# The inverse chains spaced evenly over the heads with the gate's blocks moved between them; the last two attention heads with more columns and their work shared out

## The chip, the cores and the metric

The kernel runs on one core of one Trainium2 chip. The metric is the device time of one execution in microseconds (us). The engines are TensorE (PE, with its weight loads PEld), VectorE (DVE), ScalarE (ACT), GpSimd (POOL) and SyncE (SP), which issues most DMAs. Each engine works through its own instructions in order.

## The reference

A two-layer encoder trunk over 1280 tokens of width 1024: 1024 prompt tokens and 256 sample tokens. Layer 0 is a neighbourhood attention of 16 heads of 64, its output gated by silu; layer 1 is a bidirectional gated DeltaNet of 8 heads in chunks. Cut to what matters:

```python
# layer 0, per head: window of keys, bias, softmax, weighted values; then the gate and the output projection
p = softmax(where(mask, q @ k.T + bias, NEG_INF)); o = p @ v
x = x + (o * silu(g)) @ w_out
# layer 1: projections, centred depthwise conv of 5 taps and silu on q, k, v (32 blocks of 128 channels)
proj = h @ w_in
qkv = silu(conv5(proj[..., :4096])); z = proj[..., 4096:6144]; beta, decay = ...
# per head and chunk of 64 tokens, in both directions
a_kk = tril_strict((k*beta) @ k.T * decay)
w, u = solve(I + a_kk, k*beta*exp(g)), solve(I + a_kk, v*beta)
# scan over the chunks: v_new = u - w @ S; o = q @ S + a_qk @ v_new; S = S*exp(g_last) + k.T @ v_new
y = x + (rmsnorm(o) * silu(z)) @ w_out     # then a last RMSNorm
```

## The kernel before, in words

Channels lie on partitions, tokens along the free dimension, in three token blocks of 512, 512 and 256 columns (b = 0, 1, 2). Each projection is done with weights and inputs split in a high and a low part: `proj_steps` issues for each of 8 slices of the width three matmuls (high by high, high by low, low by high, line L1176), so a block of 128 channels is 72 matmuls of 30,720 columns. `T` is 1280, `NP` 1024, `KD` 8.

The stages, by the profiled execution: attention and its output projection to about 770 us; `gdn_proj` from 770 to 1600; a transition to 1640, in which the scan's first operands are loaded (`kT`, `qT`, `vT`, L813 and on) and the last gate half runs; the scan to about 2030; the last projection and norm.

What runs beside what is set by `Side`: a generator of a piece of work is added with a delay and a pace, both counted in columns of the projection matmuls that go on meanwhile. At each projection matmul `tick(n)` adds its columns; a generator whose due time has come is advanced by one step, and its next due time is what it yields times its pace. The program so written is then laid out in a fixed order per engine, which a scheduler may still change locally, except where `keep_in_program_order` holds an instruction in its place.

**Attention.** Head h's `attention` generator (scores, softmax, transposes, product with V, gate) runs beside the projections for head h+1 (`qk_head`), the values (`v_quad`) and the gate (`g_pair`). In head 15 the projection beside it is the output projection w_o, on the part of its input that is there: `o_part(b, k)` loads what two earlier heads left in DRAM, copies it to a high part `OH` and subtracts this to get the low part `OL` (lines L337 and L340). `softmax` is a sum with a minimum on DVE (L216), an exponential on ACT (L217), a reciprocal (L218) and a scale by it (L219) on DVE. L236 transposes, L240 and L241 split the result, L256 multiplies by V, L262 to L264 apply the gate.

**gdn_proj.** 32 blocks of q, k and v channels run one after the other, f = 4h + ch: ch 0 is q, 1 is k, 2 and 3 are the halves of v. They come in the order k of head 0, then q, v, v of head h and k of head h+1. After each, ACT copies PSUM to `raw` (L487) and scales the middle tap (L490), DVE does four multiply-adds (L492), ACT a tanh (L495), DVE a product (L496), and SP stores the result (`qkv_spill`). In what follows f(h,ch) is such a block.

When a k block is there, the head's **inverse chain** `invert` is added (chain h). Its steps, in order:

- three rounds of: decay matmuls (L557), their masks on DVE (L560), exponential on ACT (L563), a store (`e_spill`), k by k matmuls on `th` (L581), DVE's products (L587, L589);
- D on ACT and DVE (L595, L596), its transpose (L605) and a mask (L606) on DVE;
- a substitution of 30 steps, each a product (L611) and a sum (L613) on DVE;
- two transposes on DVE (L617, L618), then copies into M on ACT (L626, L627) and into W and WT on POOL (L632 to L634);
- after a yield of 34000 columns the matmuls L639 of the inverse with M, ACT's copies (L642), the matmuls L646, copies on DVE (L648 to L652), matmuls L659 and L667, a copy on DVE (L669) and the store of W (`w_spill`, L670).

A chain yields 146,000 columns in all, 114,000 of them ahead of L639. The gate z of the scan's output is 16 half blocks of 128 channels, `gate_z`: projection, tanh (L519), product on DVE (L522), store (`z_spill`). In the kernel before, a chain starts 26000 columns after it is added, at pace 1 (0.92 for head 7), and after it the two z halves of head h-1 follow; z(7,0) is the last block of `gdn_proj`, and z(7,1) runs in the transition.

Of the kernel before, what the change touches and what calls it, by code (L numbers as in the profile page):

```python
# [11 lines left out]
AF = mybir.ActivationFunctionType  # L12
OP = mybir.AluOpType
# [22 lines left out]
def layer0(ctx, tc, a, h1_out):  # L36
    nc = tc.nc
# [5 lines left out]
    XH, XL = parts(xp)  # L43
# [6 lines left out]
    pp, pv = (x0.enter_context(banks(tc, n, b, "right")) for n, b in (("rms0_ps", 2), ("v0", 6)))  # L50
# [80 lines left out]
    P, V = {}, {}  # L131
# [41 lines left out]
    with st:  # L173
# [36 lines left out]
                nc.scalar.activation(G[b], t, AF.Tanh, scale=0.5)  # L210
                nc.vector.scalar_tensor_tensor(G[b], G[b], 1.0, t, op0=OP.add, op1=OP.mult)

        def softmax(S, bias, Pv):

            mx = ap.tile([128, 4], F32, name="mx", bufs=4)
            nc.vector.tensor_tensor_reduce(Pv, S, bias, -1.0, 3e38, OP.add, OP.min, mx[:, 0:1])  # L216
            nc.scalar.activation(Pv, Pv, AF.Exp, scale=-1.0, bias=mx[:, 0:1], accum_out=mx[:, 1:2])  # L217
            nc.vector.reciprocal(mx[:, 2:3], mx[:, 1:2])  # L218
            nc.vector.tensor_scalar(Pv, Pv, mx[:, 2:3], None, op0=OP.mult)  # L219

        def turned(units):

# [43 lines left out]
        def attention(h, qkk, V, G, O):  # L266

            Q, KH, KL = qkk
            bt = ap.tile([128, 896], F32, name="bias", bufs=2)
            nc.sync.dma_start(bt, a["bias_p"][h])  # L270

            def scores(p):
                own = {}
                for m in (2 * p, 2 * p + 1):
                    k0, k1 = max(m - 1, 0), min(m + 2, 8)
                    n = 128 * (k1 - k0)
                    S = ps_s.tile([128, 512], F32, name="S")[:, :n]
                    q = Q[:, 128 * m:128 * m + 128]
                    nc.tensor.matmul(S, q, KH[:, 128 * k0:128 * k1], start=True, stop=False)
                    nc.tensor.matmul(S, q, KL[:, 128 * k0:128 * k1], start=False, stop=True)  # L280
                    P = ap.tile([128, 384], F32, name="P", bufs=3)
                    b0, _ = BIAS[0 if m == 0 else 2 if m == 7 else 1]
                    softmax(S, bt[:, b0:b0 + n], P[:, :n])
                    for s in range(k0, k1):
                        own[s, m] = P[:, 128 * (s - k0):128 * (s - k0) + 128]
                    yield 800
                m = 2 * p
                edge = [(s, 128 * i, [own[s, m + i]]) for s, i in ((m - 1, 0), (m + 2, 1)) if (s, m + i) in own]
                return [[(s, 0, [own[s, m], own[s, m + 1]])] for s in (m, m + 1)] + [edge]

            def scores_s():
                bs = ap.tile([128, 2, 256], F32, name="bias_s", bufs=1)
                nc.sync.dma_start(bs, a["bias_s"][h])
                Ps = ap.tile([128, 2, 256], F32, name="Ps", bufs=1)
                S = ps_s.tile([128, 512], F32, name="S").rearrange("p (g n) -> p g n", g=2)
                for g in range(2):
                    q = Q[:, NP + 128 * g:NP + 128 * g + 128]
                    nc.tensor.matmul(S[:, g], q, KH[:, NP:], start=True, stop=False)
                    nc.tensor.matmul(S[:, g], q, KL[:, NP:], start=False, stop=True)
                    softmax(S[:, g], bs[:, g], Ps[:, g])  # L300
                yield 1600
                return [[(8 + s, 0, [Ps[:, g, 128 * s:128 * s + 128] for g in range(2)])] for s in range(2)]

            def products(j, units, ts):
                while not (j // 2 in G and all(s in V for us in units for s, _, _ in us)):
                    yield 400
                g = G[j // 2][:, 256 * (j % 2):256 * (j % 2) + 256]
                if j < 4:
                    rows = lambda t: t.rearrange("p (c r) -> p c r", r=16)
                    o = O[:, :NP].rearrange("p (r c) -> p c r", c=64)[:, 16 * j:16 * j + 16]  # L310
                    yield from pv(units, ts, V, h % 4, o, rows(g), rows)
                else:
                    yield from pv(units, ts, V, h % 4, O[:, NP:], g, lambda t: t)
                done[h] += 1

            last = None
            for j in range(5):
                units = yield from (scores(j) if j < 4 else scores_s())
                if last:
                    yield from products(*last)  # L320
                else:
                    yield 3200
                ts = yield from turned(units)
                last = j, units, ts
            yield 1600
            yield from products(*last)
            if h % 2 and h < 15:
                nc.sync.dma_start(a["o_dram"][h // 2], O)

        def o_part(b, k, late=False):  # L330

            t0, n = BLK[b]
            t = O[:, t0:t0 + n]
            if k < KD - 1:
                t = OL[k][b].bitcast(F32)
                nc.sync.dma_start(t, a["o_dram"][k, :, t0:t0 + n])
            high = nc.scalar.activation(OH[k][b], t, AF.Copy)  # L337
            if late:
                tc.keep_in_program_order(high)
            (nc.vector if k % 2 else nc.gpsimd).tensor_sub(OL[k][b], t, OH[k][b])  # L340

        done = {}
        side = Side()
        a["hi"] = True
        qkk = qk_head(0)
# [4 lines left out]
        for h in range(16):  # L350
            done[h] = 0
            G = GS[h // 2]
            V = nV if h % 4 == 0 else V
            side.add(attention(h, qkk, V, G, O), 2000, 0.75 if h in (0, 14, 15) else (1.6, 1.5, 1.5, 1.35)[h % 4])
            side.tick(0)
            q = (h + 1) // 4
            if h % 4 == 0:
                v_quad(q, V, [s for s in (4, 5) if s not in V], side)
            if h < 15:
                qkk = qk_head(h + 1, side)  # L360
            else:
                wo = [load_w(tc, a, a["w_o"][i]) for i in range(2)]
                OH, OL = parts(xp)
                begun = {(i, b): pmm.tile([128, 512], F32, name="mm")[:, :BLK[b][1]]
                         for i, b in ((0, 0), (1, 0), (0, 2))}
                for k in range(KD + 1):
                    if k < KD - 1:
                        o_part(0, k, True)
                        o_part(2, k, True)
                    if k > 1:  # L370
                        for i, b in begun:
                            for n in proj_steps(nc, begun[i, b], *wo[i], OH, OL, b, [k - 2]):
                                side.tick(n)
            if h % 4 == 0:
                v_quad(q, V, [s for s in range(10) if s not in V], side)
            if h % 4 in (1, 2) and h < 14:
                p = h // 2 + 1
                g_pair(p, GS[p], range(3), side)
            elif h % 4 == 3 and h < 15:
                nV = {}  # L380
                v_quad(q, nV, range(4), side)
            side.drain()
            if h % 2 and h < 15:
                O = ap.tile([128, T], F32, name="O", bufs=1)
# [55 lines left out]
def gdn_proj(tc, a, pmm, XH, XL):  # L440

    nc = tc.nc
    with ExitStack() as st:
# [27 lines left out]
        Z = ap.tile([128, NB, 128], F32, name="Z", bufs=1)  # L471
        for t in (D, W, WT):
            nc.gpsimd.memset(t, 0.0)
        for h, ch in [(0, 1)] + [(h + (ch == 1), ch) for h in range(8) for ch in (0, 2, 3, 1)][:-1]:
            f = 4 * h + ch
            wh, wl = a["first"].pop(0) if a["first"] else load_w(tc, a, a["w_qkv"][f])
# [20 lines left out]
            nc.sync.dma_start(a["qkv_dram"][f, :, :NP], th[:, :NP])  # L497
            nc.sync.dma_start(a["qkv_dram"][f, :, NP:], th[:, NP + 2:])
            if ch == 1:
                side.add(invert(tc, a, ap, pp, h, th, D, W, WT, Z), DELAY, 0.92 if h == 7 else 1)  # L500
            if ch == 1 and h:
                gate_z(tc, a, pmm, XH, XL, h - 1, side)
        gate_z(tc, a, pmm, XH, XL, 7, side, (0,))
        side.drain()


DELAY = 26000


def gate_z(tc, a, pmm, XH, XL, h, side, halves=(0, 1)):  # L510

    nc = tc.nc
    ws = [load_w(tc, a, a["w_z"][2 * h + i]) for i in halves]
    for i, (wh, wl) in zip(halves, ws):
        for b, (t0, n) in enumerate(BLK):
            ps = pmm.tile([128, 512], F32, name="mm")[:, :n]
            proj(nc, ps, wh, wl, XH, XL, b, side)
            z = a["zp"].tile([128, 512], F32, name="z")[:, :n]
            tanh = nc.scalar.activation(z, ps, AF.Tanh, scale=0.5)  # L519
            if h == 7:  # L520
                tc.keep_in_program_order(tanh)
            nc.vector.scalar_tensor_tensor(z, z, 1.0, ps, op0=OP.add, op1=OP.mult)  # L522
            nc.sync.dma_start(a["z_dram"][2 * h + i, :, t0:t0 + n], z)
# [907 lines left out]
```

## Time and profile before

| what | us |
|---|---|
| median of 3 runs | 2270.66 (2268.68 to 2272.76) |
| profiled execution, its own time | 2262.36 |
| its span in the profile | 2260.5 |
| granted clock of TensorE in it | 0.98 |
| PE busy | 2167.3 |
| DVE busy | 1554.3 |
| ACT busy | 1101.8 |
| POOL busy | 566.1 |

The profile is of one execution, whose time lies 8.3 us under the median. The span is what its instructions cover. "PE busy 96%" of it is a mean over all stages; PE does not wait evenly, and a stall of PE in one stage is told by the row of the instruction behind it, with the idle time and what ended it in brackets.

### The profile page before, as it was taken

What the parts mean: (1) busy time and instruction counts of PE and PEld (TensorE: products, weight loads), DVE (VectorE), ACT (ScalarE), POOL (GpSimd) and SP (SyncE); (2) the same over time, 40 slices, a digit from 0 to 9 for tenths busy, and PEclk for the clock granted to TensorE, in tenths of its full rate; (3) what the DMA queues carried; (4) which work ended last, traced back from release to release, by engine and by line L of the source; (5) the groups of instructions that cost most, each with busy time, mean ns of one, the idle gap of its engine ahead of it and who ended that gap; (6) DMA issues with size and microseconds to landing.
All of it is one profiled execution on the core that took longest, in us unless ns stands there. A gap on an engine that the chain in (4) does not pass through costs nothing.

```text
span 2260.5 us, 34062 instructions
## 1 busy us (share of the span) xinstructions
PE 2167.3 (96%) x12502; PEld 1884.9 (83%) x12502; DVE 1554.3 (69%) x3421; ACT 1101.8 (49%) x2276; POOL 566.1 (25%) x621
## 2 busy tenths in 40 slices
PE   8899999999989999999899999999899999999998
PEld 7789989889868877888778888888788888877887
DVE  6577777676772879678686887868466666676444
ACT  6454545555563553433344435344456666654233
POOL 2110110110120431312222222223176666600000
PEclk9999999999999999999899999999899999999999
DMA  6434342533646344344335354553675556567322
GB/s 190 101 80 111 83 117 73 124 92 99 171 116 183 107 114 121 104 119 127 118 91 155 98 150 125 128 148 77 192 210 164 167 183 181 145 216 236 110 96 84
DMA packets 148136, 300.10 MB, mean 133 GB/s; under 512 B 44912, under 2 KB 67440, under 8 KB 146944
## 3 DMA queue, kind: packets, MB, share of 16 engines
q1 hardware_dynamic: 126784, 232.89, 33.0%
q0 software_dynamic: 12096, 44.05, 11.0%
q10 hardware_dynamic: 9088, 20.98, 3.1%
q8 instruction: 99, 1.62, 0.3%
q14 instruction: 69, 0.57, 0.1%
HBM read 211.92 MB, written 75.45 MB: 127 GB/s over the span
## 4 chain that ended last, share of the span: by engine, by line
PE 37%; DVE 15%; DMA 3%; ACT 3%; issue 3%; POOL 1%; SPq 0%; DVEq 0%; ACTq 0%; POOLq 0%
PE mm L1176 19%; DVE acc L492 4%; DVE tmp L611 3%; DVE X L613 3%; PE k L940 3%; PE o L912 2%; PE k L931 2%; PE o L953 2%; PE u L912 2%; DMA e_spill<-E 1%; PE m L639 1%; DMA yt<-y_spill 1%; PE t L866 1%; PE m L1022 1%; DVE th L496 1%
## 5 line engine op out<-in xcount | busy, mean ns | idle before, releaser
L1176 PE MATMUL mm<-xh,wh 128*128 128x512 f32 (+1 forms) x1920 | 700.0, 365 | 4.2 <-ACT raw L487 2.0
L1176 PE MATMUL mm<-xh,wl 128*128 128x512 f32 (+1 forms) x1920 | 699.7, 364 | 2.1 <-DMA wl<-w_o 1.8
L1176 PE MATMUL mm<-xl,wh 128*128 128x512 f32 (+1 forms) x1920 | 700.1, 365 | 0.2
L1176 PEld LDWEIGHTS mm<-xh,wh 128*128 128x128 f32 x1920 | 367.1, 191 | 48.7 <-ACT raw L487 3.4
L1176 PEld LDWEIGHTS mm<-xh,wl 128*128 128x128 f32 x1920 | 367.6, 191 | 44.9 <-DMA wl<-w_o 2.2
L1176 PEld LDWEIGHTS mm<-xl,wh 128*128 128x128 f32 x1920 | 367.6, 191 | 43.7 <-DVE xl L340 0.9
L492 DVE SCALAR_TENSOR_TENSOR acc<-raw,cw,acc 128x1282 f32<-128x1282 f32 x128 | 202.2, 1579 | 38.6 <-ACT acc L490 37.2
L1126 POOL CAST wh<-wraw 128x1024 fp32r<-128x1024 f32 x32 | 34.6, 1081 | 497.7 <-PE mm L1176 442.9
L1128 ACT ACTIVATE wh<-wraw 128x1024 fp32r<-128x1024 f32 x92 | 96.8, 1055 | 93.9 <-PE mm L1176 72.8
L1176 PE MATMUL mm<-yh,wh 128*128 128x512 f32 (+1 forms) x384 | 137.5, 359 | 1.9 <-ACT yh L1050 1.7
L1176 PE MATMUL mm<-yh,wl 128*128 128x512 f32 (+1 forms) x384 | 137.0, 358 | 1.2 <-DVE wl L1130 1.2
L1176 PE MATMUL mm<-yl,wh 128*128 128x512 f32 (+1 forms) x384 | 137.6, 360 | 0.3 <-DVE yl L1051 0.3
L944 DVE TENSOR_TENSOR vl<-k,vh 128x256 fp32r<-128x256 f32 x160 | 67.0, 423 | 70.9 <-ACT vh L943 66.1
L495 ACT ACTIVATE th<-acc 128x1282 f32<-128x1282 f32 x32 | 40.9, 1277 | 152.9 <-DVE acc L492 152.9
L240 ACT ACTIVATE ph<-pt 128x512 fp32r<-128x512 f32 (+2 forms) x144 | 67.2, 478 | 78.4 <-PE pt L236 67.8
L241 DVE TENSOR_TENSOR pl<-pt,ph 128x512 fp32r<-128x512 f32 (+2 forms) x144 | 75.0, 538 | 40.8 <-ACT ph L240 39.4
L1132 ACT ACTIVATE wl<-wraw 128x1024 fp32r<-128x1024 f32 x84 | 88.7, 1056 | 14.3 <-DMA wraw<-w_qk 6.3
L217 ACT ACTIVATE P<-P,mx 128x384 f32<-128x384 f32 (+1 forms) x128 | 75.0, 586 | 41.4 <-DVE mx L216 40.1
L1192 PE MATMUL mm<-wh,xl 128*128 128x256 f32 x320 | 91.9, 287 | 0.5 <-POOL xl L65 0.4
L1192 PE MATMUL mm<-wh,xh 128*128 128x256 f32 x320 | 91.7, 288 | 0.0
L943 ACT ACTIVATE vh<-k 128x256 fp32r<-128x256 f32 x160 | 60.5, 380 | 63.6 <-PE k L940 59.8
L1192 PE MATMUL mm<-wl,xh 128*128 128x256 f32 x320 | 91.5, 286 | 0.0
(308 smaller groups left out, 4870.9 us busy)
## 6 DMA issues: line engine op xcount, KB each, us to landing
wraw<-w_qkv SPq DMA_DIRECT2D x32, 512.0 KB, 4.0
qkv_spill<-th SPq DMA_DIRECT2D x32, 512.0 KB, 2.6
wraw<-w_go SPq DMA_DIRECT2D x32, 512.0 KB, 3.5
wl<-w_qkv POOLq DMA_DIRECT2D x30, 512.0 KB, 7.3
Al<-e_spill SPq DMA_DIRECT2D x8, 1280.0 KB, 7.1
qe<-eg_spill SPq DMA_DIRECT2D x16, 640.0 KB, 8.0
wraw<-w_qk SPq DMA_DIRECT2D x16, 512.0 KB, 4.1
wl<-w_qk POOLq DMA_DIRECT2D x16, 512.0 KB, 8.7
```

What stands on the lines that cost most here:

```text
L217: nc.scalar.activation(Pv, Pv, AF.Exp, scale=-1.0, bias=mx[:, 0:1], accum_out=mx[:, 1:2])
L240: nc.scalar.activation(view(ph), view(pt), AF.Copy)
L241: nc.vector.tensor_sub(view(pl), view(pt), view(ph))
L492: nc.vector.scalar_tensor_tensor(acc, r[:, i:i + m], cw[:, f, i:i + 1], acc, op0=OP.mult, op1=OP.add)
L611: nc.vector.tensor_mul(tv, N[:, 0:c, c:c + 1].to_broadcast([128, c, n]), X[:, c:c + 1, c + 1:32].to_broadcast([128, c, n]))
L613: nc.vector.tensor_add(X[:, 0:c, c + 1:32], X[:, 0:c, c + 1:32], tv)
L912: self.tc.nc.tensor.matmul(ps, w[x], v[y], start=(first and i == 0), stop=(i == 2))
L940: nc.tensor.matmul(pw, W[:, d, cs[d]], Y[d], start=True, stop=True)
L1128: nc.scalar.activation(wh, raw, AF.Copy)
L1132: nc.scalar.activation(wl, raw, AF.Copy, scale=-1.0)
L1176: nc.tensor.matmul(ps, w[:, k, :], x[k][b], start=(k == 0 and i == 0), stop=(k == KD - 1 and i == 2))
L1192: nc.tensor.matmul(ps, x[k][b][:, cc], w[:, k % 4, :], start=(k == 0 and i == 0), stop=(k == KD - 1 and i == 2))
```

## The change

In the attention: the `attention` paces of heads 13, 14 and 15 become 1.25, 0.95 and 0.55 (1.5, 0.75 and 0.75 before); one gate block of 512 columns, 12,288 columns of matmul, is projected beside head 14 and not beside head 13; the scale of the softmax of heads 14 and 15 is on ACT; and where `o_part` runs beside head 15, the copies are on POOL and the subtractions of block 0 on POOL, of block 2 on DVE (before, copies on ACT held in program order, and subtractions on POOL and DVE in turn).

In `gdn_proj`: each chain has its own delay, the pace is 0.95, and after chain h come 1, 2, 2, 1, 2, 2, 1, 4 of the z halves, in order. So z(7,0) is the last of the four after chain 7, and the three blocks f(7,0), f(7,2), f(7,3) are the last of `gdn_proj`. Lines after the edits are 7 higher (L639 is L646, L618 is L625), L492 is L501, and L496 is L505.

```diff
-        def softmax(S, bias, Pv):
+        def softmax(S, bias, Pv, h):
...
-            nc.vector.tensor_scalar(Pv, Pv, mx[:, 2:3], None, op0=OP.mult)
+            if h < 14:
+                nc.vector.tensor_scalar(Pv, Pv, mx[:, 2:3], None, op0=OP.mult)
+            else:
+                nc.scalar.activation(Pv, Pv, AF.Copy, scale=mx[:, 2:3])
...
-        def o_part(b, k, late=False):
+        def o_part(b, k, beside=False):
...
-            high = nc.scalar.activation(OH[k][b], t, AF.Copy)
-            if late:
-                tc.keep_in_program_order(high)
-            (nc.vector if k % 2 else nc.gpsimd).tensor_sub(OL[k][b], t, OH[k][b])
+            if beside:
+                nc.gpsimd.tensor_copy(OH[k][b], t)
+                (nc.vector if b else nc.gpsimd).tensor_sub(OL[k][b], t, OH[k][b])
+            else:
+                nc.scalar.activation(OH[k][b], t, AF.Copy)
+                (nc.vector if k % 2 else nc.gpsimd).tensor_sub(OL[k][b], t, OH[k][b])
...
-            side.add(attention(h, qkk, V, G, O), 2000, 0.75 if h in (0, 14, 15) else (1.6, 1.5, 1.5, 1.35)[h % 4])
+            side.add(attention(h, qkk, V, G, O), 2000,
+                     {0: 0.75, 13: 1.25, 14: 0.95, 15: 0.55}.get(h, (1.6, 1.5, 1.5, 1.35)[h % 4]))
...
+            if h == 14:
+                g_pair(7, GS[7], (1,), side)
...
-                g_pair(p, GS[p], range(3), side)
+                g_pair(p, GS[p], range(3) if h < 13 else (0, 2), side)
...
+        zs = iter([(j // 2, j % 2) for j in range(15)])
...
             if ch == 1:
-                side.add(invert(tc, a, ap, pp, h, th, D, W, WT, Z), DELAY, 0.92 if h == 7 else 1)
-            if ch == 1 and h:
-                gate_z(tc, a, pmm, XH, XL, h - 1, side)
-        gate_z(tc, a, pmm, XH, XL, 7, side, (0,))
+                delay = (32000, 61000, 48000, 35000, 52000, 39000, 26000, 43000)[h]
+                side.add(invert(tc, a, ap, pp, h, th, D, W, WT, Z), delay, 0.92 if h == 7 else 0.95)
+                for _ in range((1, 2, 2, 1, 2, 2, 1, 4)[h]):
+                    hz, i = next(zs)
+                    gate_z(tc, a, pmm, XH, XL, hz, side, (i,))
         side.drain()
-
-
-DELAY = 26000
...
-            if h == 7:
+            if h == 7 and i:
                 tc.keep_in_program_order(tanh)
```

Where instructions move, first DVE, at the end of chain 4's substitution. In the kernel before (`raw_8843` and `raw_8844` are two of the three buffers for a block's projection, so two blocks of the convolution):

```order
1931 L613 TENSOR_TENSOR X<-X,tmp 128x2x29
1932 L611 TENSOR_TENSOR tmp<-N,X 128x30
1933 L613 TENSOR_TENSOR X<-X,tmp 128x30
1934 L617 STREAM_TRANSPOSE N<-X 128x32x32
1935 L618 STREAM_TRANSPOSE D<-X 128x32x32
1936 L492 SCALAR_TENSOR_TENSOR acc<-raw_8843,cw,acc 128x1282 x4
1937 L496 SCALAR_TENSOR_TENSOR th<-th,acc 128x1282
1938 L492 SCALAR_TENSOR_TENSOR acc<-raw_8844,cw,acc 128x1282 x4
```

And in the changed kernel at the end of the same chain's substitution:

```order
1896 L620 TENSOR_TENSOR X<-X,tmp 128x5x26
1897 L501 SCALAR_TENSOR_TENSOR acc<-raw_8844,cw,acc 128x1282
1898 L618 TENSOR_TENSOR tmp<-N,X 128x108
1899 L501 SCALAR_TENSOR_TENSOR acc<-raw_8844,cw,acc 128x1282
1900 L620 TENSOR_TENSOR X<-X,tmp 128x4x27
1901 L501 SCALAR_TENSOR_TENSOR acc<-raw_8844,cw,acc 128x1282
1902 L618 TENSOR_TENSOR tmp<-N,X 128x84
1903 L501 SCALAR_TENSOR_TENSOR acc<-raw_8844,cw,acc 128x1282
```

A block of the convolution that stood behind the chain's last transposes now stands inside its substitution. Over all chains the multiply-adds L492 between L605 and L618 were 8, 12, 12, 8, 4, 4, 4, 4 in chains 0 to 7, and are 12, 12, 12, 13, 12, 8, 12, 0.

Next SP's queue at the end of `gdn_proj`, where the scan's operands are issued. Before:

```order
356 L497 DMA qkv_spill<-th 128x1024
357 L498 DMA qkv_spill<-th 128x256
358 L523 DMA z_spill<-z 128x512 x2
359 L670 DMA w_spill<-W 128x1920
360 L523 DMA z_spill<-z 128x256
361 L781 DMA nw<-norm_w 128x2
362 L813 DMA kT<-qkv_spill 128x1280
363 L814 DMA qT<-qkv_spill 128x1280
```

And now:

```order
355 L677 DMA w_spill<-W 128x1920
356 L530 DMA z_spill<-z 128x512
357 L506 DMA qkv_spill<-th 128x1024
358 L507 DMA qkv_spill<-th 128x256
359 L1023 DMA z<-z_spill 128x2x512
360 L788 DMA nw<-norm_w 128x2
361 L820 DMA kT<-qkv_spill 128x1280
362 L821 DMA qT<-qkv_spill 128x1280
```

The store of the last block f(7,3) has come to stand between the last chain's W and the loads of kT and qT; the queue waits for it in order.

Last PE, where the scan's first operands are multiplied (L841, now L848) in the transition. Before:

```order
8086 L1176 MATMUL mm<-xl_2_7760,wh 128x256
8087 L1176 MATMUL mm<-xh_2_7736,wl 128x256
8088 L841 MATMUL t<-qT,kT 128x128 x4
8089 L1176 MATMUL mm<-xh_2_7739,wh 128x256
8090 L1176 MATMUL mm<-xl_2_7763,wh 128x256
8091 L1176 MATMUL mm<-xh_2_7739,wl 128x256
```

And now:

```order
8073 L1183 MATMUL mm<-xl_2_7778,wh 128x256
8074 L1183 MATMUL mm<-xh_2_7754,wl 128x256
8075 L848 MATMUL t<-qT,kT 128x128 x4
8076 L860 MATMUL t<-ones,q_15789 128x1 x4
8077 L865 MATMUL t<-ident,kT 128x128 x4
8078 L873 MATMUL t<-ident,vT_15716 128x128 x2
```

All of z(7,1) (x and w are its operands) stands ahead of L848 now; before, 4,608 of its columns stood behind L841.

More of the change, by code (lines that the diff above doesn't have):

```diff
@@ L282, in scores @@
                     b0, _ = BIAS[0 if m == 0 else 2 if m == 7 else 1]
-                    softmax(S, bt[:, b0:b0 + n], P[:, :n])
+                    softmax(S, bt[:, b0:b0 + n], P[:, :n], h)
                     for s in range(k0, k1):
@@ L299, in scores_s @@
                     nc.tensor.matmul(S[:, g], q, KL[:, NP:], start=False, stop=True)
-                    softmax(S[:, g], bs[:, g], Ps[:, g])
+                    softmax(S[:, g], bs[:, g], Ps[:, g], h)
                 yield 1600
```

## The prediction

> **What bounds the kernel now.** I read the page's engine shares first, then the idle time of TensorE by stretches, then its groups, then the single stalls.
>
> ```profile
> PE 2167.3 (96%) x12502; PEld 1884.9 (83%) x12502; DVE 1554.3 (69%) x3421; ACT 1101.8 (49%) x2276; POOL 566.1 (25%) x621
> ```
>
> PE is the bound: 96% of a span of 2260.5 us, so 93 us are idle. The change leaves PE's instruction count as it is; it can only move those 93 us, and the time in which the clock is at half. The stretches it touches (start:end, length, busy us of PE, PEld, DVE, ACT, POOL, granted clock, DMA share, GB/s):
>
> ```profile
> 600.00:690.00 90.00, 77.13 (x429) 63.57 (x428) 60.35 (x157) 54.43 (x120) 20.32 (x19) 0.96 0.59 171
> 770.00:1600.00 830.00, 795.71 (x4327) 688.92 (x4326) 635.74 (x1273) 358.48 (x554) 218.42 (x230) 0.97 0.43 118
> 880.00:920.00 40.00, 35.60 (x169) 30.99 (x170) 22.10 (x61) 14.88 (x27) 8.05 (x15) 0.83 0.41 115
> 1000.00:1020.00 20.00, 18.88 (x130) 17.57 (x131) 6.97 (x22) 8.60 (x18) 4.90 (x7) 0.91 0.14 55
> 1080.00:1100.00 20.00, 13.39 (x61) 11.94 (x62) 6.75 (x7) 9.45 (x18) 8.05 (x14) 0.66 0.17 59
> 1175.00:1195.00 20.00, 15.58 (x69) 13.76 (x70) 8.92 (x6) 10.54 (x18) 6.76 (x12) 0.74 0.32 84
> 1256.00:1546.00 290.00, 288.14 (x1621) 251.79 (x1620) 232.18 (x467) 129.71 (x199) 82.03 (x75) 1.00 0.49 131
> 1565.00:1585.00 20.00, 17.58 (x84) 15.97 (x84) 11.78 (x9) 8.43 (x16) 10.12 (x10) 0.74 0.09 34
> 1597.00:1640.00 43.00, 32.92 (x163) 27.44 (x162) 19.57 (x51) 17.45 (x38) 7.61 (x13) 0.76 0.75 233
> ```
>
> Attention's tail (600:690) has 12.9 us idle; the DeltaNet projection with its inverse chains (770:1600) 34.3, of which chains 4 to 6 (1256:1546) have 1.9; the transition (1597:1640) 10.1. Who is waited for in 770:1600, in PE's costliest group there, and the five stalls that make it up:
>
> ```profile
> L639 PE MATMUL m<-X,B 128*128 128x32 f32 x160 | 29.8, 309 | 20.4 <-issue 9.0 <-ACT X L626 6.0 <-POOL WT L632 5.4
> 905.26 0.39 PE L639 MATMUL m<-X,B 128*128 128x32 f32 x1 [2.00 <-ACT X L626]
> 1000.90 0.27 PE L639 MATMUL m<-X,B 128*128 128x32 f32 x1 [1.61 <-ACT X L626]
> 1086.61 0.39 PE L639 MATMUL m<-X,B 128*128 128x32 f32 x1 [8.95 <-issue]
> 1179.42 0.39 PE L639 MATMUL m<-X,B 128*128 128x32 f32 x1 [5.39 <-POOL WT L632]
> 1567.44 0.39 PE L639 MATMUL m<-X,B 128*128 128x32 f32 x1 [2.42 <-ACT X L626]
> ```
>
> 20.4 us stand before L639, a chain's first matmul after its substitution. It is the last wait there: PE is in order, so projection matmuls queue behind it. The rows are chains 0, 1, 2, 3 and 7; chains 4 to 6 have no such stall.
>
> **The change: the chains.** A chain's due time on PE is set by columns; its real readiness by DVE, which is in order too. Chain 2 (two rows) and chain 5 of before:
>
> ```profile
> 1034.63 2.18 DVE L605 STREAM_TRANSPOSE N<-D 128x1024 f32<-128x1024 f32 x1
> 1081.63 1.86 DVE L618 STREAM_TRANSPOSE D<-X 128x1024 f32<-128x1024 f32 x1
> 1313.03 0.40 PE L557 MATMUL t<-GR,one_hot 128*128 128x512 f32 x1
> 1333.76 2.18 DVE L605 STREAM_TRANSPOSE N<-D 128x1024 f32<-128x1024 f32 x1
> 1368.52 2.06 DVE L618 STREAM_TRANSPOSE D<-X 128x1024 f32<-128x1024 f32 x1
> 1375.20 0.39 PE L1176 MATMUL mm<-xh,wl 128*128 128x512 f32 x1
> 1375.43 0.30 PE L639 MATMUL m<-X,B 128*128 128x32 f32 x2
> ```
>
> From L605 to the end of L618: 48.9 and 36.8 us. In the order of before there stand 12 and 4 of the convolution's multiply-adds (L492) between them, with 2 and 1 of L496 and 0 and 1 of L522, a gate's product. By the pitch of these rows on DVE that is 28.6 + 1.46 per L492 + 1.40 per L496 + 0.6 per L522. From L618's end to L639 it is 3.1 us in chain 2, where PE waits (1083.49 to 1086.61: ACT's and POOL's copies). Chain 5 needs 20.7 us from its first L557 to L605, and is ready 60.7 us after it. PE came to its L639 after 62.4 us and 129,024 projection columns: slack 1.7. PE takes 0.23 us per 512 columns (from the row at 1375.20 to the next), so 0.45 per 1000.
>
> In the changed order chains 0 to 7 have 12, 12, 12, 13, 12, 8, 12, 0 of L492 (now L501) in that place, and 3, 3, 2, 4, 2, 2, 3, 0 of L496. The blocks that stood behind L618 in chains 3 to 6 now stand ahead of it. Ahead of L605 stand four more in chain 0 and three in chain 3. The columns from first L557 to L639 are 164,352, 141,568, 141,312, 164,864, 137,216, 130,560, 145,920, 125,952; by 62.4 + 0.45 per 1000 more, and up to 1.8 us for the matmuls L667 of the chain ahead where they now fall in between, PE gets there after 77.7, 68.5, 68.5, 78.7, 67.9, 62.7, 70.4, 60.6 us.
>
> The last L581 stands 0.6 to 1.3 us later in these chains than in chain 5, so L605 comes 21.5 us after the first L557 (22 in chain 6; 26 and 27 in chains 3 and 0). Chain 4, say: 21.5 + 28.6 + 12 x 1.46 + 2 x 1.40 + 3.2 = 73.6 against 67.9, a stall of 5.7. The same sum for all eight gives 4.6, 6.5, 5.1, 5.5, 5.7, 5.1, 5.1 and 0: 38 us before L639, for 20.4 now. To be set against it are the stalls that go, for the chains start later and off each other's backs:
>
> ```profile
> 882.39 0.58 PE L581 MATMUL t<-th 128*128 128x128 f32 x1 [4.13 <-DVE th L496]
> 988.28 0.38 PE L581 MATMUL t<-th 128*128 128x128 f32 x1 [1.61 <-DVE th L496]
> 1122.94 0.36 PE L557 MATMUL t<-GR,one_hot 128*128 128x256 f32 x1 [1.60 <-DVE E L560]
> ```
>
> 7.3 us. Idle time: 38 - 20.4 - 7.3 = **+10 us**. The bounds: if every chain were ready 1.5 us earlier, 0; 1.2 us later, +18.
>
> **The clock after stalls.** Lost is at most (1 - clock) x length: 6.8 in 880:920 (two stalls, 4.1 and 2.0), 1.8, 6.8, 5.2, 5.2 in the others, together 25.8. The 2.42 us stall of chain 7 cost as much as the 5.39 one; the 1.61 one only 1.8. The four windows with stalls of 2 us or more hold five stalls and lose 24.0: 4.8 each. Seven stalls of about 5 us: 33.6, so **+8** (from -5, if windows overlap stretches that idle anyway, to +12).
>
> The Trainium skill, "TensorE: Matmul & The Clock Gate", Part 1, What's actually happening, has the clock halve after an idle window of about 3.4 us and return after a busy one as long. Three stalls here pass 3.4 us now and seven would, which by its figures is an estimate of (7 - 3) x 3.4 / 2 = +7; the 2.42 us stall, followed by a clock of 0.74, does not fit the threshold.
>
> **The transition.** Before, the gate's half z(7,0) runs last, and f(7,3) with its convolution is long done. Its DMAs stand ahead of w_spill; then SP issues kT and qT, which the scan's first matmul L841 needs:
>
> ```profile
> 1597.35 0.32 SPq L670 DMA_DIRECT2D w_spill<-W  x1
> 1600.44 0.39 SPq L814 DMA_DIRECT2D qT<-qkv_spill  x1
> 1608.20 0.27 PE L841 MATMUL t<-qT,kT 128*128 128x128 f32 x1
> 1633.87 0.77 PE L940 MATMUL k<-V,W 128*128 128x256 f32 x1 [2.04 <-POOL W L801]
> L490 ACT ACTIVATE acc<-raw,cw 128x1282 f32<-128x1282 f32 x32 | 43.5, 1359 | 0.1
> L495 ACT ACTIVATE th<-acc 128x1282 f32<-128x1282 f32 x32 | 40.9, 1277 | 152.9 <-DVE acc L492 152.9
> qT<-qkv_spill SPq DMA_DIRECT2D x2, 640.0 KB, 4.6
> ```
>
> Now f(7,3) runs last. After its last matmul come L490 1.36, four L492 5.84, L495 1.28, L496 1.41, and for the copy out of PSUM and the handovers I allow 2 us: 12 us. Its qkv_spill then stands on SP ahead of kT and qT: from w_spill to qT SP takes 3.1 us now, and qT lands 4.6 later. L848 (L841) comes 19.8 us after f(7,3)'s end. PE has z(7,1), 30,720 columns or 13.8 us, all ahead of it; before, 4,608 of them were left behind L841 to fill the waits there. So some 6 us of idle time more ahead of L848, and no filler behind: **+6** (3 to 9).
>
> **Attention's tail.** The stalls and durations it meets:
>
> ```profile
> 619.77 0.30 PE L236 MATMUL pt<-ident,P 128*128 128x128 f32 x1 [1.76 <-DVE mx L218]
> 626.56 0.30 PE L236 MATMUL pt<-ident,P 128*128 128x128 f32 x1 [1.15 <-DVE mx L218]
> 668.02 0.38 PE L1176 MATMUL mm<-xh,wh 128*128 128x256 f32 x1 [1.83 <-ACT xh L337]
> L219 DVE TENSOR_SCALAR P<-P,mx 128x384 f32<-128x384 f32 (+1 forms) x128 | 51.2, 409 | 3.2
> 648.40 1.57 DVE L264 TENSOR_TENSOR O<-t,G 64x256 f32<-64x256 f32 x1
> 648.25 1.28 POOL L340 TENSOR_TENSOR xl<-xl,xh 128x512 fp32r<-128x512 f32 x1 [2.01 <-ACT xh L337]
> 640.20 0.41 DVE L264 TENSOR_TENSOR O<-t,G 64x256 f32<-64x256 f32 x1
> ```
>
> Head 14 gets 12,288 columns (5.5 us) from head 13: the first two stalls, 2.9 us, go. The copies of O for block 0 leave ACT, and after the last PV matmul 6,912 columns stand for 4,608: the 1.83 us go. Head 15, though, has 12,800 projection columns beside its attention, where 18,944 stood: 2.7 us less cover, near the end almost none. Its ten scales at 0.41 us (4.1 us) leave DVE for ACT; half of them lie on the chain from S to PV, so I leave 2.7 - 2.0 = +0.7. Sum: -2.9 - 1.8 + 0.7 = **-4**. Bounds: nearly all of the 12.9 us gone, -11; DVE slowed by POOL, +6: L264 took 1.57 us beside POOL's L340 and 0.41 alone, and POOL gets seven copies and seven subtractions in one run, 7 x 1.16 = 8 us against the relief.
>
> The Trainium skill, "SBUF — State Buffer", SBUF: two separate sides, says that DVE and GpSimd share a port pair which one instruction locks for its whole length. The 1.57 us beside 0.41 agree; were each of the 14 GpSimd operations to hold up DVE on the path, the tail would be an estimated +12 and not -4.
>
> **Sum.** -4 + 10 + 8 + 6 = +20 us on the profiled execution's own 2262.4, so 2282. That execution is 8.3 us under the median of the runs shown, 2270.7; a median of runs I put at **2290**. A measurement of this kernel tells 0.2%, 4.5 us, from no change.
>
> **Rivals.**
> (1) Faster. The chains come ready earlier than I add up. With a stall of x in each of seven chains the change is 7x - 27.7 of idle time, +8 of clock and +2 for the two ends: zero at x = 2.6 us. At 1.6 us a stall loses 1.8 of clock, not 4.8, and it is 11 - 28 - 13 + 2 = -28: 2243. For it: chain 5 has 1.7 us slack with four L492, and a chain that stalls hands DVE time to catch up. Against: the sum fits chains 2 and 5 of before within 0.5 us, and the stalls would have to be half of what it gives. Chance 0.15.
> (2) Lateness only changes places: x is 2.2 to 3, and the two ends cancel. 2266 to 2275; chance 0.11.
> (3) The forecast, x from 3 to 7: 2276 to 2306; chance 0.62.
> (4) More: GpSimd and DVE block each other in head 15 (+8), or the scan waits longer for f(7,3) (+9), with the chains as forecast or later: 2306 to 2322; chance 0.12.
>
> Slower 0.74, the same 0.11, faster 0.15. Leaving out 0.1 above and 0.1 below, the range is 2262 to 2308; the likeliest case alone has 2276 to 2306.
>
> **What the profile will show.** PE before L646 (L639): seven stalls of 4 to 7 us, about 38 us together, chain 7 none; each followed by a clock near 0.7. The time from L612 to the end of L625 near 49 us in chains 1, 2, 4 and 6. No stall of L588 (L581) for th. At the transition L848 some 20 us after f(7,3)'s last projection matmul, and L940 some 44 us after the last L674, for 37.2 now. I am wrong if the stalls before L646 are under 2.6 us in most chains, or if chains 4 to 6 stay as free of them as now.

## The result, and the profile after

The changed kernel takes 2312.84 us (median of 4 runs, 2307.35 to 2314.61) against 2271.65 us: a ratio of 1.0179, with a 95% interval of 1.0159 to 1.0199, so 36 to 45 us slower. Here and below a ratio is worked out over all fast runs, so it is not exactly the quotient of two medians, and one run of the kernel with attention's edits alone (3538.53 us, at a granted clock of 0.587) is not among them. The profiled execution took 2313.14 us, its span is 2311.0 us.

From the page of the changed kernel, the busy times and the granted clock in 40 slices:

```profile
PE 2192.3 (95%) x12502; PEld 1904.4 (82%) x12502; DVE 1550.6 (67%) x3402; ACT 1103.7 (48%) x2282; POOL 565.8 (24%) x634
PEclk9999999999989998999899899999899999999999
```

PE issues the same 12,502 matmuls, and is busy 25 us longer with them; the granted clock over the span is 0.965 for 0.980, some 35 us of lost clock more, part of it while PE was idle, so the clock can account for it. It is idle 118.7 us (2311.0 - 2192.3) for 93.2 before.

Both kernels have the same matmuls on PE, in another order in two stretches (attention's last heads, and `gdn_proj` with the transition). Outside these the n-th matmul is the same one in both, so the loss can be read off by stages. Time between the same counts of matmuls, with PE's idle time in brackets, in the profiles:

| stage | before | before, second profile | after |
|---|---|---|---|
| start to head 13 | 522.2 (11.2) | 522.2 (10.2) | 523.4 (10.7) |
| heads 13 to 15, start of w_o | 189.9 (13.1) | 194.8 (14.7) | 191.8 (11.8) |
| rest of w_o | 65.9 (0) | 65.9 (0) | 66.0 (0) |
| gdn_proj with the chains | 814.8 (34.3) | 814.4 (33.2) | 848.7 (50.7) |
| transition | 47.7 (10.1) | 47.7 (10.1) | 60.0 (18.6) |
| rest | 603.9 (8.8) | 603.0 (8.6) | 605.1 (11.3) |

The loss is in two places: +34 us in `gdn_proj`, of which 16.4 idle and 17.5 PE busy longer, and +12.3 in the transition (8.5 and 3.8). In windows of the changed kernel's profile (columns as in the prediction), `gdn_proj`, the transition, and stretches around four stalls:

```profile
786.00:1635.00 849.00, 798.27 (x4265) 691.46 (x4265) 619.29 (x1256) 346.76 (x541) 201.80 (x225) 0.94 0.41 113
1635.00:1695.00 60.00, 41.39 (x191) 34.72 (x189) 30.60 (x62) 20.52 (x44) 10.56 (x17) 0.74 0.65 217
1000.00:1015.00 15.00, 9.23 (x43) 8.58 (x43) 9.44 (x7) 6.88 (x14) 10.01 (x12) 0.66 0.22 64
1100.00:1120.00 20.00, 11.49 (x55) 10.51 (x56) 7.64 (x12) 10.54 (x19) 7.24 (x13) 0.66 0.16 59
1300.00:1320.00 20.00, 11.64 (x53) 10.62 (x54) 7.00 (x11) 10.52 (x18) 6.69 (x13) 0.66 0.16 60
1605.00:1620.00 15.00, 13.11 (x52) 11.74 (x53) 8.15 (x8) 4.88 (x9) 1.61 (x3) 0.66 0.11 44
```

PE's group of L646 (before: L639) in `gdn_proj`, and the rows of chains 0 to 6:

```profile
L646 PE MATMUL m<-X,B 128*128 128x32 f32 x160 | 32.5, 363 | 43.4 <-ACT X L633 25.3 <-POOL WT L639 18.1
906.05 2.92 PE L646 MATMUL m<-X,B 128*128 128x32 f32 x20 [2.98 <-ACT X L633]
1005.77 4.45 PE L646 MATMUL m<-X,B 128*128 128x32 f32 x20 [5.93 <-ACT X L633]
1108.51 4.45 PE L646 MATMUL m<-X,B 128*128 128x32 f32 x20 [9.10 <-POOL WT L639]
1218.07 4.19 PE L646 MATMUL m<-X,B 128*128 128x32 f32 x20 [4.51 <-ACT X L633]
1308.36 4.44 PE L646 MATMUL m<-X,B 128*128 128x32 f32 x20 [9.03 <-POOL WT L639]
1405.12 3.16 PE L646 MATMUL m<-X,B 128*128 128x32 f32 x14 [5.91 <-ACT X L633]
1511.09 4.45 PE L646 MATMUL m<-X,B 128*128 128x32 f32 x20 [5.92 <-ACT X L633]
```

Seven stalls, chain 7 without one, as forecast. Two of them, chains 2 and 4, are 9 us and not 5. What DVE did ahead of them stands in its rows there, and in ACT's and SP's at chain 4. The two rows at 838.67 and 940.17 are of chains 0 and 1 (in chain 1 the second round behind the first one's store):

```profile
838.67 1.13 DVE L567 SCALAR_TENSOR_TENSOR E<-t,lbG,mask 128x128 f32<-128x128 f32 x4 [1.65 <-DMA e_spill<-E]
940.17 1.13 DVE L567 SCALAR_TENSOR_TENSOR E<-t,lbG,mask 128x128 f32<-128x128 f32 x4 [2.32 <-DMA e_spill<-E]
1051.24 0.35 DVE L567 SCALAR_TENSOR_TENSOR E<-t,lbG,mask 128x128 f32<-128x128 f32 x1 [3.25 <-DMA e_spill<-E]
1251.15 0.35 DVE L567 SCALAR_TENSOR_TENSOR E<-t,lbG,mask 128x128 f32<-128x128 f32 x1 [4.05 <-DMA e_spill<-E]
1241.28 1.27 ACT L570 ACTIVATE E<-E 128x512 f32<-128x512 f32 x2
1241.40 0.33 SPq L1129 DMA_DIRECT2D wraw<-w_qkv  x1
1242.24 0.32 SPq L530 DMA_DIRECT2D z_spill<-z  x1
1242.65 10.62 SPq L583 DMA_DIRECT2D e_spill<-E  x2
```

The decay E has one buffer. The third round of a chain cannot be written before the second round's store is through, and DVE stands still until 1251.15, with the rest of the chain behind it. The store does not leave late: ACT's exponential ends at 1242.55 and SP issues it at 1242.65 (the first of the two in that row). It lands late, after 8.4 us, and after 7.9 us in chain 2; the median of these stores is 3.7 us. In both chains a load of weights (`wraw`) left SP right ahead of it, 1.2 and 0.5 us before. In the profiles of the two kernels four 512 KB stores of E stand within 1.3 us behind such a load, and all four took 7.7 to 8.5 us; that the load holds them up fits these rows, but no run moves it. In the transition, SP's queue and PE:

```profile
1645.28 0.32 SPq L506 DMA_DIRECT2D qkv_spill<-th  x1
1647.48 0.42 SPq L820 DMA_DIRECT2D kT<-qkv_spill  x1
1648.66 0.32 SPq L821 DMA_DIRECT2D qT<-qkv_spill  x1
1655.12 2.05 PE L848 MATMUL t<-qT,kT 128*128 128x128 f32 x8 [7.57 <-DMA qT<-qkv_spill]
```

f(7,3)'s store comes at 1645.28, qT 3.4 us later, and L848 6.5 us after that.

### The profile page after: what moved, and what is told of

Read it like the earlier page. It is cut to its first block, busy times and chain, and to the rows that moved or that the text cites. A ratio compares the mean times of both kernels' runs of the same rounds, so it can differ in the third digit from the quotient of the medians.

```text
span 2311.0 us, 34058 instructions
## 1 busy us (share of the span) xinstructions
PE 2192.3 (95%) x12502; PEld 1904.4 (82%) x12502; DVE 1550.6 (67%) x3402; ACT 1103.7 (48%) x2282; POOL 565.8 (24%) x634
## 4 chain that ended last, share of the span: by engine, by line
PE 62%; DVE 22%; DMA 5%; ACT 5%; issue 3%; POOL 2%; SPq 0%; DVEq 0%; ACTq 0%; POOLq 0%
PE mm L1183 34%; DVE acc L501 6%; PE mm L1199 3%; DVE X L620 3%; DVE tmp L618 3%; PE k L947 3%; PE o L919 2%; PE u L919 2%; PE k L938 2%; PE O L259 2%; PE o L960 2%; PE pt L239 2%; DVE th L505 1%; DMA e_spill<-E 1%; PE m L646 1%
## 5 line engine op out<-in xcount | busy, mean ns | idle before, releaser
L501 DVE SCALAR_TENSOR_TENSOR acc<-raw,cw,acc 128x1282 f32<-128x1282 f32 x128 | 200.1, 1563 | 15.5 <-ACT acc L499 14.5
L244 DVE TENSOR_TENSOR pl<-pt,ph 128x512 fp32r<-128x512 f32 (+1 forms) x144 | 74.8, 538 | 41.6 <-ACT ph L243 40.2
L243 ACT ACTIVATE ph<-pt 128x512 fp32r<-128x512 f32 (+1 forms) x144 | 67.0, 478 | 74.2 <-PE pt L239 64.8
L217 ACT ACTIVATE P<-P,mx 128x384 f32<-128x384 f32 (+1 forms) x128 | 75.0, 586 | 52.2 <-DVE mx L216 51.0
```

Source lines behind the costliest of these rows:

```text
L243: nc.scalar.activation(view(ph), view(pt), AF.Copy)
L244: nc.vector.tensor_sub(view(pl), view(pt), view(ph))
L501: nc.vector.scalar_tensor_tensor(acc, r[:, i:i + m], cw[:, f, i:i + 1], acc, op0=OP.mult, op1=OP.add)
```

## The experiments

Ratios are to runs of the kernel before that were taken alongside; "us" beside them is the ratio's difference from 1 times 2268. The changed kernel stands at 1.0179, +41 us.

### The parts alone

**Attention's edits alone.** `gdn_proj` and `gate_z` as before; all the diff's attention part kept.

> The edits to attention alone, on the kernel before. Theory (the parts add up, each in its own stretch): the two traces, matmul by matmul, put the attention's tail 1.9 us behind and the rest of the loss later, so 2274 us (2270 to 2278), with the chains and the transition as before. Rival (the attention's edit gains its 4 us, and the later parts hide it): 2267 us or less.

Measured: 2262.57 against 2267.77 us, 0.9981 (0.9966 to 0.9996), -4.3 us. The theory written there was wrong: it took the first profile's attention stage, 189.9 us, as typical.

**The chains' edits alone.** Attention as before; `gdn_proj` and `gate_z` as in the diff.

> The edits to gdn_proj alone, on the kernel before. Theory (the parts add up): the chains and the transition carry nearly all of it, 2310 us (2305 to 2314), with seven stalls ahead of the chains' first inverse matmul of 43 us together. Rival (attention's edit shifts what the chains meet): under 2300 us.

Measured: 2319.89 us, 1.0240 (1.0203 to 1.0277), +54 us. The chains' stage takes 849.0 us in its profile and the transition 60.0, the same as in the changed kernel (848.7 and 60.0); attention takes 195.2. So the loss is all in these edits. The times of this kernel and of the changed one differ by 13 us by the ratios, and by 3.3 us between the two profiled executions (2316.39 and 2313.14); why it is more than attention's 4 us by the ratios stays open.

**z(7,0) last again.**

```diff
-                for _ in range((1, 2, 2, 1, 2, 2, 1, 4)[h]):
+                for _ in range((1, 2, 2, 1, 2, 2, 1, 3)[h]):
...
+        gate_z(tc, a, pmm, XH, XL, 7, side, (0,))
         side.drain()
```

The tanh of both z halves of head 7 is held in program order, as in the kernel before.

> The changed kernel with z(7,0) again as the last block of gdn_proj, behind f(7,3), and three z halves after chain 7. Theory (the loss in the transition is the wait for f(7,3)'s store and qT): the 7.6 us wait of L848 goes and most of the 12.5 us that the transition lost, 2301 us (2298 to 2304). Rival (the transition is late because the clock and the scan's first operands are slow there anyway): within 4 us of the changed kernel's 2313 us.

Measured: 2293.05 us, 1.0122 (1.0090 to 1.0153), +28 us. The scan's first matmul (L848) has no wait left, and the transition takes 45.3 us for 60.0: this much of the theory holds. The time is 5 us below its range, for the transition gained 14.7 us and not most of 12.5, and the chains' stage fell too, from 848.7 to 843.9, although chain 7 now has a stall of 3.3 us.

**The delays alone, and the z halves' places alone**, each on the kernel before.

> The kernel before with the new delays and the pace 0.95 alone; two z halves stay behind each chain and z(7,0) at the end. Multiply-adds of the convolution inside the substitutions: 8, 12, 12, 8, 12, 8, 5, 10. Theory (DVE's rows against PE's columns): stalls ahead of L639 of about 2, 2, 7, 4, 7, 5, 2 and 6 us, 35 for 20, with the clock 2293 us (2285 to 2302), and nothing lost in the transition. Rival (the z halves' places cost, not the delays): 2275 us or less.

> The kernel before with the new places of the z halves alone (one to four behind each chain, f(7,3) last); delay 26000 and pace 1 for all chains. Multiply-adds inside the substitutions: 12, 8, 5, 12, 8, 4, 12, 0. Theory: stalls ahead of L639 of about 3, 3, 0, 6, 5, 0, 6 and 0 us, some 23, about as many as before; the transition loses its 12 us: 2282 us (2274 to 2290). Rival (the z halves' places cost the chains' loss too): 2300 us or more.

Measured: the delays 2299.09 us, 1.0153 (1.0126 to 1.0179), +35 us; the z halves 2284.59 us, 1.0083 (1.0063 to 1.0103), +19 us. PE's groups ahead of the chains' first inverse matmul, delays first:

```profile
L637 PE MATMUL m<-X,B 128*128 128x32 f32 x160 | 35.8, 387 | 43.0 <-ACT X L624 24.0 <-POOL WT L630 14.9 <-issue 4.1
L638 PE MATMUL m<-X,B 128*128 128x32 f32 x160 | 31.0, 328 | 24.3 <-ACT X L625 14.0 <-issue 10.3
```

The sum from the order gave 35 and 23 us. The second was 3, 3, 0, 6, 5, 0, 6 and 0 chain by chain, which fits less well than the sum; that the sum comes so near is in part luck. With the delays the stalls of chains 0 to 7 are 3.4, 4.1, 6.0, 5.6, 8.9, 5.9, 3.5, 5.6; with the z halves chains 1, 2, 3, 4 and 6 have 5.4, 1.8, 5.9, 4.9, 5.9, chain 0 has 0.4 and the others none. The z halves cost their 12 us in the transition (59.6 us, 47.7 before), and the chains under them 821.7 us for 814.8. The delays' transition took 52.2 us, where nothing was expected; why stays open. The two parts add up: 35 + 19 is the 54 of both.

### What makes L646 late

**A tile of its own for the third round's decay.**

```diff
-        E = ap.tile([128, 2, 4, 128], F32, name="E", bufs=1)[:, :, :n]
+        E = ap.tile([128, 2, 4 if n > 2 else 2, 128], F32, name="E" if n > 2 else "E3", bufs=1)[:, :, :n]
```

On the changed kernel:

> The changed kernel with a tile of its own for the decay of an inverse chain's third round, which does not wait for the second round's store (e_spill) any more. Theory (L646 is late by what DVE needs; in chains 2 and 4 DVE also stood 3 to 4 us behind that store): by the sum of the prediction for this order the stalls ahead of L646 are about 4, 4, 1, 5, 3, 4, 3 and 0 us, 24 for 43, and half of the clock loss in these chains goes with them: 2283 us (2275 to 2293). Rival (the place of L646 is moved forward as much as DVE gains): stalls of 35 us or more, 2303 us or more.

Measured: 2294.35 us, 1.0123 (1.0093 to 1.0153), +28 us. The group and chains 2 and 4:

```profile
L646 PE MATMUL m<-X,B 128*128 128x32 f32 x160 | 34.1, 361 | 35.5 <-ACT X L633 25.9 <-POOL WT L639 9.6
1088.20 0.27 PE L646 MATMUL m<-X,B 128*128 128x32 f32 x1 [4.39 <-ACT X L633]
1290.35 0.39 PE L646 MATMUL m<-X,B 128*128 128x32 f32 x1 [5.01 <-POOL WT L639]
```

Chains 2 and 4 lose their extra 4 us: 9.10 and 9.03 become 4.39 and 5.01. Chain 4 is the clean case, with 12 multiply-adds in its substitution as before; chain 2 has 8 for 12 there, so its order changed too. The other chains keep their stalls (4.6, 5.8, 4.5, 5.6, 5.6), since the order brings L646 forward as DVE gets quicker: in chain 2 from 141,312 columns after L564 to 126,976. The outcome lies between the two expectations, in stalls at the rival's edge (35.5 us), in time nearer to the theory.

**The same tile with the old chains**, with attention's edits and without:

> The attention's edits, gdn_proj as before, with the tile of its own for the third round. In this order chains 3 to 7 have 4 of the convolution's multiply-adds inside the substitution and PE comes to L639 after 124,160 to 129,024 columns. Theory (DVE's rows against PE's columns decide): the stalls of chains 2, 3 and 7 (8.9, 5.4, 2.4 us) go or fall under 2 us, with their clock loss of 17: 2236 us (2228 to 2246). Rival (the stalls come from the matmul's place, not from DVE): 2258 us or more.

> The kernel before with the tile of its own for the third round alone; attention as before. Theory (the parts add up): the gain of the attention's edits, 4 us, is missing, so 2236 us (2231 to 2241). Rival (they gain nothing): 2232 us or less.

Measured: with attention's edits 2231.90 us, 0.9843 (0.9825 to 0.9861), -36 us; without 2235.28 us, 0.9862 (0.9844 to 0.9880), -31 us. Both beat the kernel before and the changed one. The tile alone gains 31 us; the rest is attention's. From the first one's profile, `gdn_proj` in a window, the group, and its one large stall (chain 2):

```profile
789.00:1574.00 785.00, 767.36 (x4251) 666.64 (x4250) 624.65 (x1263) 347.48 (x541) 218.30 (x224) 0.98 0.45 124
L647 PE MATMUL m<-X,B 128*128 128x32 f32 x160 | 26.0, 277 | 7.5 <-ACT X L634 7.5
1073.24 0.39 PE L647 MATMUL m<-X,B 128*128 128x32 f32 x1 [5.08 <-ACT X L634]
```

Here the order keeps 4 multiply-adds in the substitutions of chains 3 to 7, and PE comes to them after 124,160 to 129,024 columns: none of them waits. Chain 2, which was to fall under 2 us, keeps 5.08. The 31 us are not of the waits for E alone, for the order changed with the tile: chains 2 and 3 have 8 and 4 multiply-adds in their substitutions for 12 and 8 in the kernel before. No run keeps the old order with the new tile.

**L646 later.** On the changed kernel, its first matmul held in program order:

```diff
-    yield 34000
+    yield 34000 + (14000, 22000, 26000, 15000, 30000, 16000, 18000, 0)[h]
...
+        if c == 0:
+            tc.keep_in_program_order(first)
```

The three later yields of a chain, 8000, 16000 and 8000, are 3000 each in chains 0 to 6.

> The changed kernel with L646 held in program order and due 14,000 to 30,000 columns later in chains 0 to 6 (the later steps of the chain correspondingly shorter), so that PE comes to it 10,000 to 18,000 columns later in chains 1, 2, 4 and 5, with 3 multiply-adds more inside chain 1's and 3's substitution. Theory (DVE's rows against PE's columns, from the stalls measured in the changed kernel): stalls of about 3, 5, 6, 4, 4, 0, 6 and 0 us, 28 for 43; with the clock 2293 us (2285 to 2301). Rival (L646 waits about 5.5 us wherever it is put, since the order already follows an estimate of when M is ready): stalls as now, 2307 us or more.

Measured: 2295.77 us, 1.0129 (1.0108 to 1.0151), +29 us.

```profile
L646 PE MATMUL m<-X,B 128*128 128x32 f32 x160 | 33.4, 338 | 28.4 <-ACT X L633 23.7 <-POOL WT L639 4.7
1310.34 0.39 PE L646 MATMUL m<-X,B 128*128 128x32 f32 x1 [3.75 <-ACT X L633]
```

28.4 us of stalls for the 28 worked out, which started from the stalls of the changed kernel; chain by chain 4.4, 4.7, 6.6, 3.1, 3.8, 0, 6.0, 0 for 3, 5, 6, 4, 4, 0, 6, 0. So the stall follows DVE's rows against PE's columns; the rival, a fixed lateness, falls with chains 4 and 5.

**All three mended**, on the changed kernel: the third tile, L646 later (in chain 7 too, by 8000 columns), z(7,0) last.

> The changed kernel with three things at once: the tile of its own for the third round, L646 due later as in the run before, and z(7,0) as the last block. Theory (the three losses add up): stalls ahead of L646 of about 5, 1, 1, 5, 0, 0, 5 and 0 us, and the transition as with z(7,0) last: 2252 us (2242 to 2262), faster than the kernel before, slower than the old delays with the third tile (2232). Rival (spaced chains keep a loss that these three don't hold): 2265 us or more.

Measured: 2271.11 us, 1.0022 (1.0009 to 1.0035), +5 us: the rival. The stalls ahead of the first inverse matmul did fall to 16.1 us, but another took their place:

```profile
L647 PE MATMUL m<-X,B 128*128 128x32 f32 x160 | 29.5, 292 | 16.1 <-POOL WT L640 9.3 <-ACT X L634 6.8
L656 PE MATMUL m<-X,Z 128*128 128x32 f32 x160 | 28.8, 290 | 9.8 <-ACT Z L652 9.6
781.00:1606.00 825.00, 791.03 (x4266) 685.33 (x4265) 625.81 (x1264) 347.93 (x542) 205.63 (x227) 0.95 0.43 117
```

With the later steps of a chain 3000 columns apart, the next matmul (L656) waits for ACT's copy Z, 9.8 us in all. The likely reading is that a chain fills the distance to the next one as it is, so that time given to one step is taken from another; no run tests it. As an estimate, at the 0.7 us of clock per us of idle time found at the end of this document, the 9.8 us cost some 17 of the 19 us by which the time lies above the 2252 worked out; the transition took 48.8 us, 3.5 more than with z(7,0) last alone.

### The clock, and the kernel before again

**Filled.** On the changed kernel, ahead of the first matmul of L646:

```diff
+    for _ in range((21, 41, 64, 31, 63, 41, 41, 0)[h]):
+        nc.tensor.matmul(zt, a["one_hot"][:, h, None].to_broadcast([128, 128]), a["GR"][:, :32 * NB], ...)
```

> The changed kernel with extra matmuls (0.14 us each, 320 columns, their result overwritten) ahead of each chain's first inverse matmul: 21, 41, 64, 31, 63, 41, 41 and 0 in chains 0 to 7, so that TensorE works while it waits; in chains 1, 2, 4 and 5 they stand right ahead of it, in 0, 3 and 6 partly 20 to 60 matmuls earlier. Theory (an idle TensorE loses its clock, and that costs about as much as the wait itself): the waits stay and the half clock after them goes in chains 1, 2, 4 and 5 at least, 24 us of 43, so 2288 us (2278 to 2296). Rival (the half clock costs little, since DVE is what is late anyway): 2313 us or more.

Measured: 2338.28 us, 1.0308 (1.0279 to 1.0336), +70 us, slower than the changed kernel. Chain 1 in PE's rows, and the two groups:

```profile
993.18 6.12 PE L646 MATMUL m<-GR,one_hot 128*128 128x320 f32 x41
1005.62 0.39 PE L648 MATMUL m<-X,B 128*128 128x32 f32 x1 [5.85 <-ACT X L633]
L646 PE MATMUL m<-GR,one_hot 128*128 128x320 f32 x302 | 45.2, 308 | 0.0
L648 PE MATMUL m<-X,B 128*128 128x32 f32 x160 | 33.9, 337 | 35.2 <-ACT X L633 23.9 <-POOL WT L639 11.3
```

The filling did not fill the wait: the order counted it and put less projection ahead (in chain 1 128,256 columns for 141,568, where the filling has 13,120), so PE still came 5.85 us early, and of 43.4 us of stalls 35.2 were left. The run says nothing on the clock; what it shows is that extra work ahead of L646 displaces other work. Whether a stall's clock loss could be had back by itself stays open.

**The kernel before, again.**

> The kernel before, unchanged, profiled once more. Theory (its first profile was of a quick execution, above all in attention's tail): the time lies within 0.3% of the other runs of before, and the stretch of attention's heads 13 to 15 and w_o, 189.9 us in the first profile, takes 192 to 196; heads 13 to 15 with the edits took 189.2 to 193.2. Rival (the attention's edits gain nothing there): 190 to 191 us again.

Measured: 1.0009 (0.9995 to 1.0023); attention's heads 13 to 15 take 194.8 us, the chains and the transition 814.4 and 47.7 (the table above). The row that differs from the first profile's 1.76 us:

```profile
621.87 0.45 PE L236 MATMUL pt<-ident,P 128*128 128x128 f32 x1 [4.56 <-DVE mx L218]
```

With the old attention that stage took 189.9, 195.2, 192.3, 194.4, 194.8 and 190.5 us in six profiles, mean 192.9; with the edits 191.8, 193.2, 191.9, 189.2, 191.2, 191.3 and 188.4 in seven, mean 191.0 (the filled kernel has other counts and is left out). The 1.9 us between the means are less than the spread of either.

## Why the prediction was wrong

The direction and the mechanism were right, the size was half: +20 us forecast, +41 measured, 5 us above the range. What failed are three sizes in the sum: DVE's time from L557 to L605, which left out the waits for the store of E; the clock's price for the stalls; and the transition, where qT landed later. The time falls in rival (4)'s range, not by the first of its two mechanisms, and by the second only in part. Term by term:

- **Attention's tail, -4: right by the runs.** -4.3 us alone (-7.7 to -0.9), and 2235.28 against 2231.90 with the third tile. The named stalls went, and one of 1.30 us came ahead of L259 (L256 before). By the profiles the stage gains 1.9 us, which is not clear of their spread. The Trainium skill, "SBUF — State Buffer", SBUF: two separate sides, says that DVE and GpSimd share a port pair that one instruction locks for its whole length. Single rows agree: of 80 rows of DVE's L264 those that overlap no POOL instruction take 0.64 us at most, those that do up to 1.57 (1.52 in the changed kernel). The edits did not make it worse: from 600 to 690 us the row takes 698 ns on average, for 763 before. The 0.41 us that the prediction calls alone is the shortest of these rows; alone they take 0.58 on average.
- **Idle time of the chains, +10: +16.4.** The sum ahead of L646 gave 38 us, and 43.4 came. The term that was mis-sized is L557 to L605 (now L564 to L612). It took 29.9, 23.8, 26.8, 28.1, 28.0, 21.9 and 23.8 us in chains 0 to 6, where I had 27, 21.5, 21.5, 26, 21.5, 21.5 and 22. In chains 2 and 4 DVE waited 3.25 and 4.05 us for the store of E, a wait that the prediction nowhere had. It was there to read, in DVE's group of L560 in the profile of before:

```profile
L560 DVE SCALAR_TENSOR_TENSOR E<-t,lbG,mask 128x128 f32<-128x128 f32 x160 | 45.1, 343 | 12.8 <-DMA e_spill<-E 12.7
```

  12.7 us over the eight chains, of which the chain that I calibrated by had its share of 1.4 us. In the new order there are 12.1, on four chains: 2.5, 2.3, 3.3 and 4.1 us in chains 0, 1, 2 and 4. The run with the third tile took them away in chains 2 and 4, and the two stalls fell by 4.7 and 4.0. In chains 0 and 1 the waits did not lengthen the stall, because PE too came later there than I worked out, by 3.5 and 2.8 us (by 3.1 in chain 4 and 0.1 to 1.7 in the others); what delayed it is not worked out here. The pitch of the substitution held (50.3, 48.9, 48.8 and 50.3 us in chains 1, 2, 4 and 6). Stalls worked out in this manner came out as 28.4 for 28, 24.3 for 23, 43.0 for 35 us, the last again with 8.9 us in chain 4, and 35.5 for 24 with the third tile, where the order brought L646 forward. The stalls that were to go (4.13, 1.61, 1.60) went; 1.8 us at a z product and 3.0 us ahead of L653 came new, and some 4 us of smaller stalls went. Rival (1)'s own sum is zero at 2.5 us a stall, not 2.6; nothing hangs on it.
- **Clock, +8: +17.5**, or +11 against the profile of attention's edits alone, whose same chains were busy 787.1 us. I took 4.8 us of lost clock for each stall ahead of L646; by windows of 5 us the seven lost 42.6, some 6 each (5.1 in 1000:1015 and 6.8 in 1100:1120, at a clock of 0.66) and from 3.4 in chain 3 to 10.2 in chain 0, and the new 3.0 us stall ahead of L653 lost 5.1 as well (1605:1620), which the term didn't count. Part of that time PE was idle anyway: over all of `gdn_proj` the clock lost some 51 us for 25 before. No run removes the lost clock alone, so this term is read from the profiles and not tested.
- **Transition, +6: +12.3.** f(7,3)'s store came 11.9 us after its last matmul (12 forecast) and qT left SP 3.4 us later (3.1 forecast). But it was 6.5 us from there to L848, not 4.6, so the wait was 7.57 us; and the clock after it, which I left out of this term, cost 3.8. From the last L674 to L947 it is 48.2 us for the 44 forecast.
- **8 us between the profiled execution and the median: right** to add. 4.9 of them lay in attention's stage, by the second profile of before.

Of the signs named these came: seven stalls, none in chain 7, each followed by a clock below 0.8; 48.8 to 50.3 us from L612 to the end of L625 in chains 1, 2, 4 and 6; no stall for th. The sizes of three stalls (3.0, 9.1 and 9.0 us) and the 48.2 us were outside; L848 came 21.7 us after f(7,3)'s last matmul, for some 20.

## What to carry to other kernels

A stall of an in-order engine that stands where an order written by estimate meets another engine's real pace can be worked out before the run: count the other engine's rows in between, and price each by its pitch. But count the waits of those rows too: a single buffer with a store behind it (E) is a row of the sum, and here one more tile of 2 KB per partition gained 31 us in the old order and 13 in the new one, against 41 lost by moving work about. A term for idle time on TensorE needs its clock term beside it, here of nearly the same size.

## What the runs showed of the hardware

In `gdn_proj` the same matmuls keep PE busy 766 to 768 us in the two kernels with 18 to 19 us of idle time, 780 to 791 with 32 to 35, and 786 to 798 with 39 to 55: a straight line through the thirteen profiles (the filled kernel left out) rises by 0.7 us of busy time per us of idle time, with a scatter of several us. The loss hardly follows a stall's length: a stall of 2.97 us and one of 5.93 cost 5.1 us each by the windows, one of 9.1 us 6.8, and those of chains 0 and 3, 2.98 and 4.51 us, cost 10.2 and 3.4. Windows of the changed kernel around these two, and from the end of chain 2's stall:

```profile
905.00:930.00 25.00, 23.95 (x107) 22.32 (x107) 4.42 (x10) 7.88 (x18) 2.58 (x5) 0.59 0.06 22
1215.00:1230.00 15.00, 11.94 (x63) 10.78 (x64) 3.05 (x7) 5.55 (x13) 5.31 (x11) 0.77 0.15 56
1108.51:1115.90 7.39, 7.39 (x28) 6.71 (x29) 0.00 (x0) 4.50 (x8) 1.66 (x4) 0.50 0.10 38
```

These losses are multiples of 1.7 us. The Trainium skill, "TensorE: Matmul & The Clock Gate", Part 1, What's actually happening, gives a window of about 3.4 us, half of which is 1.7: this agrees. That one busy window brings full speed back does not agree: after chain 2's stall PE was busy for 7.39 of 7.39 us at a clock of 0.50.
